# Trace of a batched matrix product: the order of five-row and twelve-row loads

## The chip, the cores and the metric

The kernel runs on one core of a Trainium2 chip. The metric is the device time of one execution in microseconds (us).

## The reference

```python
B, N = 8, 2176
a, b = randn(B, N, N), randn(B, N, N)          # float32

def reference(a, b):
    prod = np.matmul(a, b)
    traces = np.diagonal(prod, axis1=1, axis2=2).sum(axis=-1)
    return traces.astype(np.float32)           # 8 numbers
```

No product of matrices is needed: the trace of A B is the sum over all i, k of A[i, k] B[k, i], so each batch is an elementwise product of A transposed with B, summed. Both inputs, 2 x 8 x 2176 x 2176 float32 or 303 MB, have to be read once.

## The kernel before, in words

**Rows and tiles.** A matrix has 17 row tiles of 128 rows. They are held in three groups of 6, 6 and 5: in a group with m rows a partition holds m neighbouring rows of the matrix, so that a load is one long run in each partition. `a_six` and `b_six` hold the first two groups (twelve rows a partition) of A and of B, and **one** buffer, `five`, holds the last group of A and, later, the last group of B. `at` holds A transposed. All four are single buffers in bf16. In what follows a "row" is one such row tile, 128 x 2176, and a load has twelve, six or five rows.

**Loads.** POOL issues all loads but one, with a cast from float32 to bf16 on the way, into a single queue. Its program is a list written by hand: waits and `fetch` calls (L179) in a fixed order. In batch 0 the first row of A comes over SP's queue as float32 into the space of `b_six` (`words`) and is cast by ScalarE and VectorE. The waits that free the buffers are: `made` (TensorE has transposed so many tiles) ahead of a load over A's rows, and `product` (VectorE has finished so many products) ahead of a load over B's. `five` changes hands twice a batch: A's five rows go in after the product with B's five rows, B's five rows after all tiles of A's five rows are made.

**TensorE** runs the same program for each batch: 26 tiles (`EACH`), each of them up to 16 transposes into one of three PSUM slots (L224 for pairs of bf16 columns moved as float32, L227 for bf16). The 18 tiles of the twelve rows come first (`HEAD` = 18), then the 8 tiles of the five rows. It waits on `moved` at tiles 0 and `HEAD`; SP waits for the loads of A in that order and posts the counts (L173).

**Emptying the slots.** ScalarE copies three tiles of four from PSUM to `at` (L269), VectorE the fourth (L295). Before its first tile of a batch each waits for both products of the batch before, as these still read `at`.

**Products.** VectorE multiplies and sums `at` with B (L284): with the twelve rows of B, then with the five.

**The last batch.** B arrives in nine pieces (`pieces`), the twelve rows as 6, 4 and 2, the five as 2, 1, 1 and three parts of a row. VectorE takes some pieces, TensorE others as matrix products whose diagonals add up in `trace_ps` (L253); filler matmuls (L255) lie between these. Then the parts are summed, and SP stores the eight results.

The order of POOL's issues before is, for batch n: A's twelve rows, A's five rows, B's twelve rows, B's five rows.

Of the kernel before, what the change touches and what calls it, by code (L numbers as in the profile page):

```python
# [21 lines left out]
def kernel(  # L22
# [7 lines left out]
    P = 128  # L30
    BATCH, N, N2 = a.shape
    assert N == N2 and N % P == 0
    NT = N // P
    SIX, FIVE = 6, 5
    TWICE = 2 * SIX
    assert TWICE + FIVE == NT
    LAST = BATCH - 1
# [12 lines left out]
    a_six = big.tile([P, TWICE, N], bf16, tag="a_six")  # L50
    b_six = big.tile([P, TWICE, N], bf16, tag="b_six")
    five = big.tile([P, FIVE, N], bf16, tag="five")
# [14 lines left out]
    def tiles_of(rows, start, m):  # L67
# [31 lines left out]
    six_tiles = [  # L99
        t for g in range(2)  # L100
        for t in tiles_of(a_six[:, g * SIX:(g + 1) * SIX, :], g * SIX * P, SIX)
    ]
    five_tiles = list(tiles_of(five, TWICE * P, FIVE))
    tiles = six_tiles + five_tiles
    EACH, HEAD = len(tiles), len(six_tiles)
    on_vector = [n for n in range(EACH) if n % 4 == 3]
    on_scalar = [n for n in range(EACH) if n % 4 != 3]

    def flat(t):
        return t.rearrange("p r k -> p (r k)")  # L110

    def six(src):
        return src[0:TWICE * P, :].rearrange("(g p r) k -> p g (r k)", g=2, r=SIX)

    def rows_of(src, start, m, r0, r1):
        return src[start:start + P * m, :].rearrange("(p r) k -> p (r k)", r=m)[:, r0 * N:r1 * N]

    by_twos = "p (g r) k -> p g (r k)"
# [29 lines left out]
    with tc.tile_critical(no_gpsimd_drain=True) as section:  # L148
        def counted(name):
            return Counted(nc, name)  # L150

        first_row, first_five = counted("first_row"), counted("first_five")
        d_a6, d_a5, d_b6, d_b5 = (counted(f"load_{x}") for x in ("a6", "a5", "b6", "b5"))
        d_late = [counted(f"late{n}") for n in range(len(pieces))]
        zeros, ready, cast = counted("zeros"), counted("ready"), counted("cast")
        moved, made = nc.alloc_semaphore("moved"), nc.alloc_semaphore("made")
        free = [nc.alloc_semaphore(f"free{k}") for k in range(SLOTS)]
        scalar_done, vector_done = counted("scalar_done"), counted("vector_done")
        product, early, added = counted("product"), counted("early"), counted("added")
# [3 lines left out]

        sp = nc.sync
        words = flat(b_six[:, 0:2, :].bitcast(f32))
        first_row.by(sp.dma_start(out=words, in_=rows_of(a[0], 0, SIX, 0, 1)), 16)
        for n in range(BATCH):
            if n == 0:
                sp.wait_ge(cast.sem, 2)
                sp.wait_ge(first_five.sem, 16)  # L170
            for load in (d_a6, d_a5):
                sp.wait_ge(load.sem, 16 * (n + 1))
                sp.sem_inc(moved)  # L173


        gp = nc.gpsimd

        def fetch(count, dst, src):
            count.by(gp.dma_start(out=dst, in_=src), 16)  # L179

        for n in range(BATCH):
            if n == 0:
                fetch(first_five, flat(a_six[:, 1:SIX, :]), rows_of(a[0], 0, SIX, 1, SIX))
                fetch(d_a6, flat(a_six[:, SIX:, :]), rows_of(a[0], SIX * P, SIX, 0, SIX))
                gp.wait_ge(zeros.sem, 2)
                for t in (identity32, identity16):
                    ready.by(gp.affine_select(
                        out=t, in_=t, compare_op=mybir.AluOpType.not_equal, fill=1.0, base=0,
                        pattern=[[-1, P]], channel_multiplier=1,
                    ))  # L190
            else:
                gp.wait_ge(made, EACH * (n - 1) + HEAD)
                fetch(d_a6, a_six.rearrange(by_twos, g=2), six(a[n]))
                gp.wait_ge(product.sem, 2 * n)
            fetch(d_a5, flat(five), rows_of(a[n], TWICE * P, FIVE, 0, FIVE))
            if n == 0:
                gp.wait_ge(cast.sem, 2)
            else:
                gp.wait_ge(product.sem, 2 * n - 1)
            if n < LAST:  # L200
                fetch(d_b6, b_six.rearrange(by_twos, g=2), six(b[n]))
                gp.wait_ge(made, EACH * (n + 1))
                fetch(d_b5, flat(five), rows_of(b[n], TWICE * P, FIVE, 0, FIVE))
                continue
            for k, piece in enumerate(pieces):
                if piece.v0 == TWICE:
                    gp.wait_ge(made, EACH * (n + 1))
                fetch(d_late[k], piece.dst, piece.src)
        gp.drain()


        pe = nc.tensor
# [2 lines left out]
            pe.sem_inc(free[k])  # L215
        with pe.Fori(0, BATCH):
            for n, (moves, _, _) in enumerate(tiles):
                if n in (0, HEAD):
                    pe.wait_ge(moved, 1).then_inc(moved, -1)
                ps = slots[n % SLOTS]  # L220
                pe.wait_ge(free[n % SLOTS], 1).then_inc(free[n % SLOTS], -1)  # L221
                for dtype, place, src in moves:
                    if dtype == f32:
                        last = pe.transpose(ps[:, place, :], src, identity32)  # L224
                    else:
                        ps16 = ps.bitcast(bf16).rearrange("q a b -> q (a b)")
                        last = pe.transpose(ps16[:, place * P:(place + 1) * P], src, identity16)  # L227
                last.then_inc(made, 1)
# [18 lines left out]
        for w in work:  # L247
            k, x, y = w
# [10 lines left out]
        middle = N // 2  # L259
        act = nc.scalar  # L260
        act.wait_ge(first_row.sem, 16)
        cast.by(act.copy(out=a_six[:, 0, :middle], in_=words[:, :middle]))  # L262
        for n in range(BATCH):
            for t in on_scalar:
                _, dst, view = tiles[t]
# [10 lines left out]
        dve = nc.vector  # L276
# [1 line left out]
        for t in (identity32, identity16):  # L278
            zeros.by(dve.memset(t, 0.0))
        dve.wait_ge(first_row.sem, 16)  # L280
        cast.by(dve.tensor_copy(out=a_six[:, 0, middle:], in_=words[:, middle:]))  # L281

        def multiply_reduce(x, y, acc, out=None):
            return dve.tensor_tensor_reduce(  # L284
                out=x if out is None else out, in0=x, in1=y, scale=1.0, scalar=0.0,
                op0=MUL, op1=ADD, accum_out=acc,
            )

        for n in range(BATCH):
            for t in on_vector:  # L290
                _, dst, view = tiles[t]
                if t == on_vector[0] and n:
                    dve.wait_ge(product.sem, 2 * n)
                dve.wait_ge(made, EACH * n + t + 1)
                ins = dve.tensor_copy(out=dst, in_=view(slots[t % SLOTS]))  # L295
                if t != on_vector[-1]:
                    ins.then_inc(free[t % SLOTS], 1)
                else:
                    vector_done.by(ins)
            dve.wait_ge(vector_done.sem, n + 1).then_inc(free[on_vector[-1] % SLOTS], 1)  # L300
            dve.wait_ge(scalar_done.sem, n + 1).then_inc(free[on_scalar[-1] % SLOTS], 1)
            if n == LAST:
                continue
            for k, (load, t, v0) in enumerate(((d_b6, b_six, 0), (d_b5, five, TWICE))):
                dve.wait_ge(load.sem, 16 * (n + 1))
                product.by(multiply_reduce(
                    flat(at[:, v0:v0 + t.shape[1], :]), flat(t), sums[:, 2 * n + k:2 * n + k + 1],
                ))
        dve.wait_ge(early.sem, 1)
        dve.reduce_sum(  # L310
            out=result[:1, 0:LAST],
            in_=total[:, 0:2 * LAST].rearrange("o (b n) -> o b n", n=2),
# [3 lines left out]
        for k, (piece, (lo, hi, _)) in enumerate(zip(pieces, shares)):  # L316
            if hi > lo:
                dve.wait_ge(d_late[k].sem, 16)
                t, base = (b_six, 0) if piece.v0 < TWICE else (five, TWICE)
# [11 lines left out]
        for c in range(cols):  # L331
# [9 lines left out]
            out=out.rearrange("(a b) -> a b", a=1), in_=result[:1, :],  # L341
# [40 lines left out]
```

## Time and profile before

| | |
|---|---|
| median of 3 runs | 709.66 us (709.39 to 709.72) |
| profiled execution | 709.2 us, its span 707.1 us |
| busy share: VectorE, ScalarE, TensorE, POOL | 54%, 29%, 26%, 4% |
| POOL's queue, share of 16 DMA engines | 99.7%, 7552 packets, 150.96 MB written |
| read from HBM | 303.04 MB, 429 GB/s over the span |
| product with twelve rows of B, with five | 27.36 us, 11.48 us |
| granted TensorE clock, mean | 0.671 |

The span runs from the first to the last instruction. In the profile PE is TensorE, PEld its weight loads, DVE VectorE, ACT ScalarE, POOL GpSimd and SP SyncE, and L179 is line 179 of the kernel. Instructions that issue a DMA are not counted as busy time of the engine; a DMA's own time is on the queues. "idle before <-" names what ended the time in which an engine waited.

### The profile page before, as it was taken

The page shows a single profiled execution, that of the slowest core. Times are in us where ns is not written, and L with a number is a line of the kernel's source. Part 1 is how long each engine was busy: PE and PEld are TensorE (multiplying, and loading weights), DVE is VectorE, ACT ScalarE, POOL GpSimd, SP SyncE. Part 2 cuts the span into 40 slices and gives each one's busy share as a digit, 9 for nine tenths or more (in the row PEclk, how much of TensorE's full clock was granted, in tenths as well). Part 3 has the DMA queues.
Part 4 walks back from the last instruction along what each step waited for, and adds up shares of the span by engine and source line. Part 5 has one row for each costly group of instructions (what it writes and reads, how often), then busy time and mean ns, then how long its engine had stood idle before and what let it go on. Part 6 is the DMA issues. An engine that isn't in the chain of part 4 may idle for free. (4 is left out here: it accounts for less than half of the span.)

```text
span 707.1 us, 3879 instructions
## 1 busy us (share of the span) xinstructions
PE 182.3 (26%) x1611; PEld 164.0 (23%) x1613; DVE 380.7 (54%) x94; ACT 203.8 (29%) x162; POOL 24.9 (4%) x46
## 2 busy tenths in 40 slices
PE   0083000830018200182002710028100371003706
PEld 0073000730017200172002610027000370003704
DVE  0031596315963169541794407944089340894487
ACT  1095000950009400093001930019200292003910
POOL 1000000000000000000000000000000000001010
PEclk9998555885559755597555965559655596555957
DMA  9999999999999999999999999999999999999997
GB/s 221 222 219 212 213 228 203 216 219 216 219 215 220 219 215 217 211 217 222 220 213 217 220 217 214 220 213 221 217 215 213 219 222 213 220 219 213 218 209 152
DMA packets 7702, 152.13 MB, mean 215 GB/s; under 512 B 658, under 2 KB 914, under 8 KB 1298
## 3 DMA queue, kind: packets, MB, share of 16 engines
q0 software_dynamic: 7552, 150.96, 99.7%
q1 hardware_dynamic: 146, 1.11, 0.5%
q8 instruction: 2, 0.03, 0.0%
q14 instruction: 2, 0.02, 0.0%
HBM read 303.04 MB, written 0.00 MB: 429 GB/s over the span
## 5 line engine op out<-in xcount | busy, mean ns | idle before, releaser
L269 ACT COPY at<-aT 128x1536 bf16<-128x1536 bf16 (+3 forms) x160 | 201.4, 1367 | 465.5 <-PE aT L224 465.1
L284 DVE CUSTOM_DVE_ANT_0 at<-at,b_six 128x26112 bf16<-128x26112 bf16 (+2 forms) x9 | 214.4, 23831 | 130.9 <-DMA b_six<-in_b_dram 130.9
L224 PE MATMUL aT<-identity,a_six 128*128 128x128 f32 x576 | 91.6, 324 | 482.6 <-PEq L221 482.6
L224 PEld LDWEIGHTS aT<-identity,a_six 128*128 128x128 f32 x576 | 85.4, 207 | 488.1 <-issue 487.8
L295 DVE COPY at<-aT 128x1536 bf16<-128x1536 bf16 (+1 forms) x48 | 80.1, 1669 | 182.7 <-PE aT L224 152.0
L284 DVE CUSTOM_DVE_ANT_0 at<-at,five 128x10880 bf16<-128x10880 bf16 (+3 forms) x10 | 85.0, 8501 | 1.6 <-DMA five<-in_b_dram 1.6
L227 PE MATMUL aT<-identity,a_six 128*128 128x128 bf16 x480 | 33.5, 219 | 11.6 <-PEq L221 11.4
L224 PE MATMUL aT<-identity,five 128*128 128x128 f32 x240 | 34.6, 289 | 4.4 <-PEq L221 4.4
L227 PEld LDWEIGHTS aT<-identity,a_six 128*128 128x128 bf16 x480 | 29.3, 118 | 15.5 <-issue 15.4
L224 PEld LDWEIGHTS aT<-identity,five 128*128 128x128 f32 x240 | 30.4, 198 | 7.4 <-issue 7.0
L179 POOL DMA_DIRECT2D five<-in_a_dram x8 | 4.4, 556 | 389.0 <-DVE sums L284 389.0
L179 POOL DMA_DIRECT2D five<-in_b_dram x13 | 7.1, 555 | 256.5 <-PE aT L227 256.5
L227 PE MATMUL aT<-identity,five 128*128 128x128 bf16 x200 | 13.9, 219 | 2.8 <-PEq L221 1.8
L227 PEld LDWEIGHTS aT<-identity,five 128*128 128x128 bf16 x200 | 11.9, 118 | 5.1 <-issue 5.1
L253 PE MATMUL trace_ps<-b_six,at 128*128 128x128 bf16 x34 | 3.8, 310 | 18.3 <-DMA b_six<-in_b_dram 18.3
L253 PEld LDWEIGHTS trace_ps<-b_six,at 128*128 128x128 bf16 x34 | 3.5, 145 | 18.4 <-issue 18.4
L179 POOL DMA_DIRECT2D b_six<-in_b_dram x10 | 6.6, 662 | 3.6 <-ACT a_six L262 3.6
L179 POOL DMA_DIRECT2D a_six<-in_a_dram x9 | 6.2, 687 | 1.0 <-SPq L148 1.0
L253 PE MATMUL trace_ps<-five,at 128*128 128x128 bf16 x54 | 3.8, 220 | 2.6 <-DMA five<-in_b_dram 2.4
L253 PEld LDWEIGHTS trace_ps<-five,at 128*128 128x128 bf16 x54 | 3.0, 98 | 4.4 <-DMA five<-in_b_dram 4.3
L255 PE MATMUL aT<-at 128*128 128x512 bf16 x13 | 3.7, 412 | 0.3 <-issue 0.2
L281 DVE CAST a_six<-b_six 128x1088 bf16<-128x1088 f32 x1 | 0.7, 726 | 4.7 <-DMA b_six<-in_a_dram 4.7
(19 smaller groups left out, 8.6 us busy)
## 6 DMA issues: line engine op xcount, KB each, us to landing
b_six<-in_b_dram POOLq DMA_DIRECT2D x7, 6528.0 KB, 47.7
a_six<-in_a_dram POOLq DMA_DIRECT2D x7, 6528.0 KB, 60.9
five<-in_a_dram POOLq DMA_DIRECT2D x8, 2720.0 KB, 17.4
five<-in_b_dram POOLq DMA_DIRECT2D x7, 2720.0 KB, 30.7
a_six<-in_a_dram POOLq DMA_DIRECT2D x1, 3264.0 KB, 32.1
b_six<-in_b_dram POOLq DMA_DIRECT2D x1, 3264.0 KB, 32.3
a_six<-in_a_dram POOLq DMA_DIRECT2D x1, 2720.0 KB, 17.3
b_six<-in_b_dram POOLq DMA_DIRECT2D x1, 2176.0 KB, 42.0
```

The source lines that it names most:

```text
L179: count.by(gp.dma_start(out=dst, in_=src), 16)
L224: last = pe.transpose(ps[:, place, :], src, identity32)
L227: last = pe.transpose(ps16[:, place * P:(place + 1) * P], src, identity16)
L253: ins = pe.matmul(trace_ps, x, y, start=w is real[0], stop=w is real[-1])
L255: pe.matmul(slots[0][:, 0:4, :], x, y, start=True, stop=True)
L269: ins = act.copy(out=dst, in_=view(slots[t % SLOTS]))
L281: cast.by(dve.tensor_copy(out=a_six[:, 0, middle:], in_=words[:, middle:]))
L284: return dve.tensor_tensor_reduce(out=x if out is None else out, in0=x, in1=y, scale=1.0, scalar=0.0, op0=MUL, op1=ADD, accum_out=acc,)
L295: ins = dve.tensor_copy(out=dst, in_=view(slots[t % SLOTS]))
```

## The change

For each batch the five-row loads are issued ahead of the twelve-row loads, for A and for B: A's five, A's twelve, B's five, B's twelve. TensorE's tiles follow: the 8 tiles of the five rows first (`HEAD` = 8), then the 18 of the twelve. VectorE multiplies with B's five rows first. In batch 0 SP's row is now the first of A's five, POOL loads the other four and then all twelve rows in one load (before: five, six, five). In the last batch A's twelve rows come as two loads of six, and TensorE waits a third time in each batch, at tile 17 (`SECOND`), for the second of them; in the other batches SP posts two counts when the twelve rows have landed. The waits ahead of each load are changed to suit: A's five rows wait for the first product of the batch before, A's twelve for all its tiles, B's five for the first eight tiles of this batch, B's twelve for the second product of the batch before.

```diff
--- before.py
+++ after.py
@@ -101,8 +101,9 @@
         for t in tiles_of(a_six[:, g * SIX:(g + 1) * SIX, :], g * SIX * P, SIX)
     ]
     five_tiles = list(tiles_of(five, TWICE * P, FIVE))
-    tiles = six_tiles + five_tiles
-    EACH, HEAD = len(tiles), len(six_tiles)
+    tiles = five_tiles + six_tiles
+    EACH, HEAD = len(tiles), len(five_tiles)
+    SECOND = HEAD + len(six_tiles) // 2
     on_vector = [n for n in range(EACH) if n % 4 == 3]
     on_scalar = [n for n in range(EACH) if n % 4 != 3]
 
@@ -149,8 +150,9 @@
         def counted(name):
             return Counted(nc, name)
 
-        first_row, first_five = counted("first_row"), counted("first_five")
+        first_row = counted("first_row")
         d_a6, d_a5, d_b6, d_b5 = (counted(f"load_{x}") for x in ("a6", "a5", "b6", "b5"))
+        d_half = [counted(f"half{g}") for g in range(2)]
         d_late = [counted(f"late{n}") for n in range(len(pieces))]
         zeros, ready, cast = counted("zeros"), counted("ready"), counted("cast")
         moved, made = nc.alloc_semaphore("moved"), nc.alloc_semaphore("made")
@@ -163,50 +165,61 @@
 
         sp = nc.sync
         words = flat(b_six[:, 0:2, :].bitcast(f32))
-        first_row.by(sp.dma_start(out=words, in_=rows_of(a[0], 0, SIX, 0, 1)), 16)
+        first_row.by(sp.dma_start(out=words, in_=rows_of(a[0], TWICE * P, FIVE, 0, 1)), 16)
+
+
+
+        gp = nc.gpsimd
+        arrivals = []
+
+        def fetch(count, dst, src, opens=0):
+            reached = count.by(gp.dma_start(out=dst, in_=src), 16)
+            if opens:
+                arrivals.append((count.sem, reached, opens))
+
         for n in range(BATCH):
             if n == 0:
-                sp.wait_ge(cast.sem, 2)
-                sp.wait_ge(first_five.sem, 16)
-            for load in (d_a6, d_a5):
-                sp.wait_ge(load.sem, 16 * (n + 1))
-                sp.sem_inc(moved)
-
-
-        gp = nc.gpsimd
-
-        def fetch(count, dst, src):
-            count.by(gp.dma_start(out=dst, in_=src), 16)
-
-        for n in range(BATCH):
+                fetch(d_a5, flat(five[:, 1:FIVE, :]), rows_of(a[0], TWICE * P, FIVE, 1, FIVE), 1)
+            else:
+                gp.wait_ge(product.sem, 2 * n - 1)
+                fetch(d_a5, flat(five), rows_of(a[n], TWICE * P, FIVE, 0, FIVE), 1)
+                gp.wait_ge(made, EACH * n)
+            if n < LAST:
+                fetch(d_a6, a_six.rearrange(by_twos, g=2), six(a[n]), 2)
+            else:
+                for g in range(2):
+                    fetch(
+                        d_half[g], flat(a_six[:, g * SIX:(g + 1) * SIX, :]),
+                        rows_of(a[n], g * SIX * P, SIX, 0, SIX), 1,
+                    )
             if n == 0:
-                fetch(first_five, flat(a_six[:, 1:SIX, :]), rows_of(a[0], 0, SIX, 1, SIX))
-                fetch(d_a6, flat(a_six[:, SIX:, :]), rows_of(a[0], SIX * P, SIX, 0, SIX))
                 gp.wait_ge(zeros.sem, 2)
                 for t in (identity32, identity16):
                     ready.by(gp.affine_select(
                         out=t, in_=t, compare_op=mybir.AluOpType.not_equal, fill=1.0, base=0,
                         pattern=[[-1, P]], channel_multiplier=1,
                     ))
-            else:
-                gp.wait_ge(made, EACH * (n - 1) + HEAD)
-                fetch(d_a6, a_six.rearrange(by_twos, g=2), six(a[n]))
-                gp.wait_ge(product.sem, 2 * n)
-            fetch(d_a5, flat(five), rows_of(a[n], TWICE * P, FIVE, 0, FIVE))
-            if n == 0:
-                gp.wait_ge(cast.sem, 2)
-            else:
-                gp.wait_ge(product.sem, 2 * n - 1)
             if n < LAST:
+                gp.wait_ge(made, EACH * n + HEAD)
+                fetch(d_b5, flat(five), rows_of(b[n], TWICE * P, FIVE, 0, FIVE))
+                if n == 0:
+                    gp.wait_ge(cast.sem, 2)
+                else:
+                    gp.wait_ge(product.sem, 2 * n)
                 fetch(d_b6, b_six.rearrange(by_twos, g=2), six(b[n]))
-                gp.wait_ge(made, EACH * (n + 1))
-                fetch(d_b5, flat(five), rows_of(b[n], TWICE * P, FIVE, 0, FIVE))
                 continue
+            gp.wait_ge(product.sem, 2 * n)
             for k, piece in enumerate(pieces):
                 if piece.v0 == TWICE:
-                    gp.wait_ge(made, EACH * (n + 1))
+                    gp.wait_ge(made, EACH * n + HEAD)
                 fetch(d_late[k], piece.dst, piece.src)
         gp.drain()
+
+
+        sp.wait_ge(cast.sem, 2)
+        for sem, reached, opens in arrivals:
+            sp.wait_ge(sem, reached)
+            sp.sem_inc(moved, opens)
 
 
         pe = nc.tensor
@@ -215,7 +228,7 @@
             pe.sem_inc(free[k])
         with pe.Fori(0, BATCH):
             for n, (moves, _, _) in enumerate(tiles):
-                if n in (0, HEAD):
+                if n in (0, HEAD, SECOND):
                     pe.wait_ge(moved, 1).then_inc(moved, -1)
                 ps = slots[n % SLOTS]
                 pe.wait_ge(free[n % SLOTS], 1).then_inc(free[n % SLOTS], -1)
@@ -259,7 +272,7 @@
         middle = N // 2
         act = nc.scalar
         act.wait_ge(first_row.sem, 16)
-        cast.by(act.copy(out=a_six[:, 0, :middle], in_=words[:, :middle]))
+        cast.by(act.copy(out=five[:, 0, :middle], in_=words[:, :middle]))
         for n in range(BATCH):
             for t in on_scalar:
                 _, dst, view = tiles[t]
@@ -278,7 +291,7 @@
         for t in (identity32, identity16):
             zeros.by(dve.memset(t, 0.0))
         dve.wait_ge(first_row.sem, 16)
-        cast.by(dve.tensor_copy(out=a_six[:, 0, middle:], in_=words[:, middle:]))
+        cast.by(dve.tensor_copy(out=five[:, 0, middle:], in_=words[:, middle:]))
 
         def multiply_reduce(x, y, acc, out=None):
             return dve.tensor_tensor_reduce(
@@ -301,7 +314,7 @@
             dve.wait_ge(scalar_done.sem, n + 1).then_inc(free[on_scalar[-1] % SLOTS], 1)
             if n == LAST:
                 continue
-            for k, (load, t, v0) in enumerate(((d_b6, b_six, 0), (d_b5, five, TWICE))):
+            for k, (load, t, v0) in enumerate(((d_b5, five, TWICE), (d_b6, b_six, 0))):
                 dve.wait_ge(load.sem, 16 * (n + 1))
                 product.by(multiply_reduce(
                     flat(at[:, v0:v0 + t.shape[1], :]), flat(t), sums[:, 2 * n + k:2 * n + k + 1],
```

## The prediction

> **What bounds the kernel now.** I read the page first: engine shares, slices, queues. The columns of the slices are fortieths of the span, 17.7 us each.
>
> ```profile
> span 707.1 us, 3879 instructions
> ...
> DVE  0031596315963169541794407944089340894487
> ...
> DMA  9999999999999999999999999999999999999997
> GB/s 221 222 219 212 213 228 203 216 219 216 219 215 220 219 215 217 211 217 222 220 213 217 220 217 214 220 213 221 217 215 213 219 222 213 220 219 213 218 209 152
> ...
> q0 software_dynamic: 7552, 150.96, 99.7%
> ```
>
> No compute engine reaches 60% of the span (VectorE 54%, the most), while the DMA row holds 9 in all slices but the last and one queue, POOL's, fills 99.7% of 16 engines' time. So the bytes bound the kernel, and an edit can gain only where that queue runs dry, or ahead of its first byte, or behind its last. Next the chain of waits of the end, in order of time:
>
> ```profile
> 672.25 2.08 POOL five L179 x4
> 674.33 29.41 DMA five<-in_b_dram
> 703.74 0.04 issue
> 703.79 0.61 PE trace_ps L253 x6
> ```
>
> The last pieces of B are issued at 672.25 and land at 703.74, behind others in the queue. About 3.3 us follow to the end of the span (707.06 - 703.74): last matmuls, trace, store.
>
> Then the timeline around the issues of batch 1, to see how full the queue is when POOL refills it (start, duration, idle before):
>
> ```profile
> 106.19 11.48 DVE L284 CUSTOM_DVE_ANT_0 at<-at,five 128x10880 bf16<-128x10880 bf16 x1
> 117.60 0.08 DVE L284 DVE_READ_ACCUMULATOR2_ANT sums<- 128x1 f32 x1
> 117.97 0.56 POOL L179 DMA_DIRECT2D five<-in_a_dram  x1 [56.24 <-DVE sums L284]
> 118.53 0.71 POOL L179 DMA_DIRECT2D b_six<-in_b_dram  x1
> 122.85 0.30 PEld L224 LDWEIGHTS aT<-identity,a_six 128*128 128x128 f32 x2 [62.84 <-issue]
> 122.88 0.45 PE L224 MATMUL aT<-identity,a_six 128*128 128x128 f32 x1 [62.72 <-PEq L221]
> ```
>
> PE starts as the twelve rows of A land (122.88). The five-row load behind them was issued at 117.97, a **lead** of 4.91 us. In the batches after it the same two rows give 4.91 (210.33 - 205.42), 4.91, 4.91, 4.86, 4.88, 4.86. Is that enough? The windows between these issues:
>
> ```profile
> 117.90:205.40 87.50, 21.65 (x187) 19.87 (x187) 48.79 (x10) 25.21 (x20) 2.53 (x4) 0.64 1.01 215
> 205.40:292.70 87.30, 20.96 (x187) 19.05 (x187) 48.79 (x10) 25.12 (x20) 2.53 (x4) 0.64 1.01 217
> 292.70:380.00 87.30, 21.53 (x187) 19.62 (x187) 48.79 (x10) 25.21 (x20) 2.53 (x4) 0.64 1.01 217
> ```
>
> A batch takes 87.45 us from issue to issue the first time (205.42 - 117.97), then 87.29; DMA share is 1.01. So 34 rows of tiles cost 87.29 us: 2.567 a row, 12.84 for a five-row load, 15.40 for six, 30.81 for twelve. A lead of 4.9 is just enough: the trace's packet records show packets of the late five-row load starting 2.7 us after its issue in batch 1, as the twelve-row load's packets run out.
>
> **The bytes.** Before, batch 0's A is 1 + 5 + 6 + 5 rows, after it 1 + 4 + 12: both 17. The last batch's twelve rows become 6 + 6. Loads: before 6 + 6x4 + 11 = 41, after 5 + 6x4 + 12 = 41. Every packet is a run of one partition, and the packet records have a fixed time per size (26,112 bytes 1942 ns, 21,760 1622, 17,408 1302, which is 320 ns a row and 22 more). Batch 0 has three groups of packets either way, 1622 + 1942 + 1622 = 5186 before and 1302 + 2 x 1942 = 5186 after. Cost 0.
>
> **The start.** SP's first row and POOL's first load keep their places ahead of all else; the first POOL load is shorter by one row, 2.57 us, and the twelve-row load behind it is issued within 1.2 us of it (the two first issues take 1.20). POOL now issues batch 0's loads of B only when the five-row tiles of A are made: those rows land at about 34.3 - 15.4 - 2.6 = 16.3 (the first twelve rows landed at 34.3; six rows and one less), and the tiles take 7.3 (below), so at about 24 instead of 7.39. What hides this is the queue: it holds 17 rows, 44 us, from the beginning. Without that cover it would cost about 17 us once. Cost 0.
>
> **The steady batches.** Let b be the landing of B's twelve rows of the batch before.
> - *Issue of B's five rows.* The next A, 17 rows, lands at b + 43.98 (122.88 - 78.90). VectorE now does the short product first, so the long one runs from b: 27.36 and 0.08. Only then may ScalarE and VectorE write `at`, so the five rows of A, which land at b + 13, wait about 14 us and gain nothing by being early. TensorE has three slots filled by then. Eight five-row tiles took 7.3 us from PE's first (53.16) to the issue that waited for them (60.46); with three tiles ready I take the same 7.3 as the upper end and ScalarE's five copies of 1.27 to the slot of tile 7, 6.4, as the lower. Issue at b + 27.4 + 0.4 + 7.3 = b + 35.1. Lead 43.98 - 35.1 = 8.9 us, where 4.9 was just enough. B's twelve rows follow 0.6 us later: the product they wait for is over.
> - *Issue of A's five rows.* From the landing of A's twelve rows, 18 tiles take 18.3 us (34.68 to 53.0), ScalarE's last copy 2.0, the short product 11.48, POOL 0.4: 32.2. B lands at 43.47 (166.35 - 122.88). Lead 11.3 us. The twelve rows of A follow at once, since all tiles were transposed before that product.
>
> Both leads are about double those of before. What can be gained is what the queue lost: at least nothing, at most the dip in slice 6, (217 - 203)/217 x 17.7 = 1.1 us; by the periods 87.45 - 87.29 = 0.16, and 0.27 over all six (641.98 - 117.97 = 524.01 against 6 x 87.29 = 523.74). I take -0.3, near the periods, since single slices scatter by 10 GB/s.
>
> **The rule against it.** When the eighth five-row tile is made, POOL issues B's loads while VectorE copies that tile; no issue inside a batch of before lies under a VectorE instruction. The copies take 1492 ns for 1280 elements and 1758 for 1536, 1.04 ns an element. If such a copy held the issue up, it would take at most 1.49 of the 8.9 us, which leaves 7.4; that decides nothing alone, and together with slower tiles it is 2 of the 7 in 100 of rival 1. The Trainium skill, "SBUF — State Buffer", section "SBUF: two separate sides", says that GpSimd cannot write the descriptors of its DMAs while VectorE runs an instruction in a mode that takes both ports. By it, too, the sum would stay where it is; no row here shows such a stall.
>
> **PE's waits.** A third wait, at tile 17, is added to each batch; but for the last, SP posts two counts when the twelve rows land, so it finds its count at once. SP's own waits stand in order of arrival, with nothing of its own queued behind them but the final store. Cost 0.
>
> **The last batch.** A's last load lands at 659.4 in both:
>
> ```profile
> L173 SPq EVENT_SEMAPHORE  x16: 17/17/28, 34.3 to 659.4; - x16
> ```
>
> After, that load is six rows: nine tiles, 9.2 us, and 2.0 for ScalarE give 670.6, where before VectorE was free at 674.2 and the first piece of B landed at 674.8. So VectorE again waits for the load. Had the twelve rows stayed one load, it would be 659.4 + 18.3 + 2.0 = 679.7, 4.9 late, and VectorE's pieces (13.8, 9.2, 2.4, 1.4, 0.8 us, with 1.6 us of waits between them: 1.0, 0.2, 0.4) would end some 3 us late: the split hides that. The pieces of B keep order and size; they are issued from about 642 on, the five-row ones about 649 instead of 672.25, with the queue full. Cost 0, and behind the last byte nothing changes.
>
> **Sum.** 709.2 (the profiled execution; its span and 2.1 around it) - 0.3 = 708.9. The median of the runs is 0.46 above that execution: 709.4.
>
> **Rivals.**
> 1. *The queue runs dry at B's five-row load.* Place: POOL's wait for the eighth tile, behind a 27.4 us product. It decides when the product and tiles together end later than b + 39, that is if the eight tiles take over 11.3 us rather than 7.3. For it: PE's clock is 0.5 after its idle time, and this load had not stood behind the long product. Against: 36 transposes took 6.92 us from a cold start in batch 1, and ScalarE's copies, not PE, set the pace. Each us too late costs seven batches 7 us: one us gives 716.4. 7 in 100.
> 2. *The gaps were larger than the periods show*, and the lead of 4.9 cost the queue a little in every batch. For: slice 6. Against: 87.29 comes again to 0.1 us in five batches, with no slice like it. Full dip 1.1: 708.6. If each of seven batches lost 0.4 us: 709.66 - 2.8 = 706.9. 15 in 100 for the first kind, which is still within 0.2%; 6 for the second.
> 3. *One DMA engine falls behind elsewhere.* From 34.68 to 122.88, 34 rows too, took 88.20, 0.9 above 87.29. The packet records show two instruction packets of 16 KB beside the loads, 935 and 974 ns, at 54 and 694. Who is last at the end depends on which engine they hit: both on one, up to 1.0 more, 710.4. 12 in 100; no rival of size, but the upper end of the range.
> 4. *The change does not do what it says*: the five rows come early, but `at` is not free. I count this as certain, and it is in the sum.
>
> **Numbers.** Sum as it stands, or within half a us of it, 57 in 100; large dip 15, engine behind 12: these 84 are within 0.2% (1.42 us), which is about what a measurement of this kernel can tell from no change. Slower: rival 1 with 7, and 3 for what I have not seen, 10. Faster 6. The range goes from the full dip, 708.5, to the sum with an engine 1.0 behind and 0.3 for gaps that stay, 710.7.
>
> **What would show it.** In the profile after: DMA 9 in all slices but the last; a period of 87.3 between POOL's issues; POOL waiting for PE before B's five rows, with a lead of some 9 us, and 11 us at A's five rows; VectorE idle ahead of the long product, not the short; the last landing near 703.5. Wrong if VectorE's long product starts at intervals above 87.5 (rival 1), below 87.1 (rival 2), or if PE's last transposes pass 674.

## The result and the profile after

The change makes the kernel faster by about a microsecond: 708.11 us (707.97 to 708.24, 20 runs) against 709.21 us (708.36 to 709.72, 20 runs). The ratio is 0.9985 with a 95% interval of 0.9979 to 0.9991, which is 0.6 to 1.5 us. That is within the 0.2% called no change, but below the low end of the range, 708.5. The runs also lie closer together: 0.27 us from lowest to highest instead of 1.36.

The page of the profiled execution after (708.12 us, span 706.0), the same lines:

```profile
span 706.0 us, 3887 instructions
...
DVE  0105488054871549715396163961639616395477
...
DMA  9999999999999999999999999999999999999997
GB/s 225 225 208 211 226 214 215 216 225 213 216 227 213 206 219 221 215 213 227 209 218 228 210 210 226 214 215 214 226 207 219 228 207 214 224 217 215 213 213 159
...
q0 software_dynamic: 7552, 150.96, 99.7%
```

The queue is as full as before by this view: packets, bytes and share are the same. The slices scatter more than before (206 to 228 without the last), though nothing runs dry any more, and the first experiment below, in which nothing runs dry either, has 205 in the very slice that reads 203 before. So that slice, on which the bound of 1.1 us rested, is no measure of a gap. The chain of waits of the end, in order of time:

```profile
650.50 1.56 POOL five L176 x3
652.06 49.97 DMA five<-in_b_dram
702.03 0.05 issue
702.08 0.51 PE trace_ps L266 x6
702.59 0.07 another core or an unknown queue
702.66 0.04 issue
702.70 0.62 PE trace_ps L266 x6
```

The last wait for a piece of B that the chain shows ends at 702.66 instead of 703.74, and that is the whole gain: span 706.0 instead of 707.1. (Both chains merge the wait for the very last piece into the matmuls; it lands at 702.98 and 704.06, also 1.08 us apart.) B's five-row pieces are issued at 650.50, not 672.25, and wait 50 us in the queue.

The timeline at the two places where the queue is refilled, first B's loads of batch 1:

```profile
121.85 1.49 DVE L308 COPY at<-aT 128x1280 bf16<-128x1280 bf16 x1 [2.82 <-PE aT L237]
...
125.58 1.49 DVE L308 COPY at<-aT 128x1280 bf16<-128x1280 bf16 x1 [2.25 <-PE aT L240]
125.84 0.56 POOL L176 DMA_DIRECT2D five<-in_b_dram  x1 [45.14 <-PE aT L240]
126.41 0.71 POOL L176 DMA_DIRECT2D b_six<-in_b_dram  x1
135.61 2.43 PEld L237 LDWEIGHTS aT<-identity,a_six 128*128 128x128 f32 x12 [10.22 <-issue]
135.64 2.59 PE L237 MATMUL aT<-identity,a_six 128*128 128x128 f32 x11 [10.09 <-PEq L234]
```

then A's loads of batch 2:

```profile
167.95 0.56 POOL L176 DMA_DIRECT2D five<-in_a_dram  x1 [40.84 <-DVE sums L297]
168.51 0.71 POOL L176 DMA_DIRECT2D a_six<-in_a_dram  x1
178.94 27.36 DVE L297 CUSTOM_DVE_ANT_0 at<-at,b_six 128x26112 bf16<-128x26112 bf16 x1 [11.29 <-DMA b_six<-in_b_dram]
```

The leads are 9.80 us (135.64 - 125.84; 8.7 to 10.0 in the six batches) and 10.99 us (178.94 - 167.95), where there was one of 4.9. VectorE now waits 11.3 us ahead of the long product and none of it matters.

What the page can't show is in the trace's records of single packets. A packet of a five-row load, 21,760 bytes, takes 1622 ns. Just after POOL's late five-row load of A reached the queue in batch 1, at 120.7 us of the kernel before, 18 of them took 1680 to 2624 ns. I read this as a dry spell: DMA engines had run out of packets and waited for the new ones. Each row sums what such stretched packets took above 1622 ns and divides it by the 16 engines:

```
                      excess per DMA engine, us (time of the spell)
before                0.40 (120.7)  0.05 (208.3)  0.04 (295.6)  0.02 (644.9)
after                 none at any refill
```

### The profile page after: what moved, and what is told of

The parts are those of the page before. It is cut to its first block, busy times and chain, and to the rows that moved or that the text cites. A ratio compares the mean times of both kernels' runs of the same rounds, so it can differ in the third digit from the quotient of the medians.

```text
span 706.0 us, 3887 instructions
## 1 busy us (share of the span) xinstructions
PE 203.7 (29%) x1611; PEld 184.7 (26%) x1613; DVE 381.4 (54%) x94; ACT 204.9 (29%) x162; POOL 25.1 (4%) x46
## 3 DMA queue, kind: packets, MB, share of 16 engines
q0 software_dynamic: 7552, 150.96, 99.7%
q1 hardware_dynamic: 146, 1.11, 0.5%
## 5 line engine op out<-in xcount | busy, mean ns | idle before, releaser
L237 PE MATMUL aT<-identity,five 128*128 128x128 f32 x240 | 54.7, 418 | 367.7 <-PEq L234 367.7
L237 PEld LDWEIGHTS aT<-identity,five 128*128 128x128 f32 x240 | 47.0, 221 | 373.6 <-issue 373.6
L240 PE MATMUL aT<-identity,five 128*128 128x128 bf16 x200 | 17.1, 260 | 0.1
L240 PEld LDWEIGHTS aT<-identity,five 128*128 128x128 bf16 x200 | 16.8, 132 | 0.7 <-issue 0.3
```

## The experiments

Theory: the lead of 4.9 us is at the edge, the queue runs dry there, and the longer leads of the change prevent it. Rival: the gain lies in batch 0's loads, in the last batch's order or in where packets of code fall. Medians of the kernel before in the four groups of runs: 708.84 (first two experiments), 709.13 (next four), 708.87 and 708.63.

**The old order with a longer lead.** Only the size of the long product is changed:

```diff
+                rows = 10 if k == 0 else t.shape[1]
...
-                    flat(at[:, v0:v0 + t.shape[1], :]), flat(t), sums[:, 2 * n + k:2 * n + k + 1],
+                    flat(at[:, v0:v0 + rows, :]), flat(t[:, 0:rows, :]),
+                    sums[:, 2 * n + k:2 * n + k + 1],
```

> The kernel before, its loads and tiles in the old order; VectorE's long product leaves out two of the twelve rows of B (4.6 us shorter), so that the lead of A's five-row load grows from 4.9 to 9.5 us. Theory (the queue ran dry at that load, and engines that ran dry lost up to 1 us): faster than before by what the change gained, 0.7 to 1.2 us. Rival (the gain lies in batch 0's loads or in the last batch's order, not in the lead): within 0.2 us of before.

708.20 us, ratio 0.9989 (0.9980 to 0.9998), all runs from 707.98 to 708.31: the time of the kernel after, and its narrow spread, with none of its order. No stretched packets at any refill. So the start and the last batch of the change add nothing to the gain that can be measured, and the lead is the cause.

**The same in batch 0 alone** (`rows = 10 if k == 0 and n == 0`).

> The kernel before; two of the twelve rows are left out of the long product in batch 0 alone, so that only batch 1's five-row load of A is issued 4.6 us earlier. Theory: the dry spell at 120.7 us is by far the largest, so this has most of the gain, 0.5 to 1.0 us. If instead every batch lost a little: a seventh of the gain, 0.15 us. Rival (start or end of the kernel): nothing.

708.92 us, ratio 0.9999 (0.9990 to 1.0008): no gain, a miss. The trace says where it went. In batch 1 the lead is long, in batch 2 it is 4.91 again:

```profile
113.43 0.56 POOL L179 DMA_DIRECT2D five<-in_a_dram  x1 [52.19 <-DVE sums L284]
...
122.87 1.52 PE L224 MATMUL aT<-identity,a_six 128*128 128x128 f32 x6 [63.19 <-PEq L221]
```
```profile
205.25 0.56 POOL L179 DMA_DIRECT2D five<-in_a_dram  x1 [55.65 <-DVE sums L284]
...
210.16 3.23 PE L224 MATMUL aT<-identity,a_six 128*128 128x128 f32 x14 [62.12 <-PEq L221]
```

The stretched packets are gone at 120.7 and stand at 208.1 us instead (0.19 us an engine). The spell is not tied to batch 1; it comes at the first refill with the short lead. (This execution took 708.25 us and is one of the faster of its 11 runs, so its spell need not be what the median lost.) The reason is in the landings, where each of the 16 DMA engines posts its own count. In before, one engine falls 1.0 us behind the other 15 after a packet of code (16 KB, 935 ns, at 54 us, in the profile's queue q8): for A's twelve rows of batch 1, 15 counts come from 120.99 to 121.57 us and the last at 122.56. VectorE's product starts when that last engine has landed, so POOL's refill is late by 1.0 us for the other 15. Once they have run dry they stand closer to the laggard (five of them within 0.6 us of it at the next landing), and later refills cost less.

**A lead longer by 1.2 us**, the size of that lag (long product without 1150 of its 26112 elements):

> The kernel before; the long product leaves out 1150 of 26112 elements, about 1.2 us, so that the lead grows from 4.9 to 6.1 us. In the traces one DMA engine lags the rest by 1.0 us after a packet of code, and the product starts when that engine has landed, so that the other 15 run dry once by up to 1.0 us less what the lead has to spare. Theory: 1.2 us more are just enough to cover that lag, and the kernel comes to within 0.3 us of the one with the lead of 9.5 (708.2). Rival (every batch wants a long lead): at most a third of that gain.

708.13 us, ratio 0.9987 (0.9978 to 0.9996).

```profile
116.91 0.56 POOL L179 DMA_DIRECT2D five<-in_a_dram  x1 [54.89 <-DVE sums L284]
...
123.01 1.31 PE L224 MATMUL aT<-identity,a_six 128*128 128x128 f32 x5 [62.56 <-PEq L221]
```

A lead of 6.1 us is enough for the whole gain, and its trace has no stretched packets at the refills. Leads of 9 and 11 us buy no more.

**A shorter lead, in the old order and in the new.** Ahead of the second product of a batch (`k == 1`), VectorE does a spare one, of 800 elements in the old order and of 4352 in the new:

```diff
+                if k == 1:
+                    x = flat(t)[:, 0:SPARE]
+                    multiply_reduce(x, x, late[:, 7:8], out=spare)
```

> The kernel before; ahead of each short product VectorE squares 800 elements of B's five rows into a spare tile, about 1.0 us, so that the lead of A's five-row load falls from 4.9 to about 3.9 us in seven batches. Theory (4.9 is just enough, and the loss counts once for an engine that lags but in every batch for a lead that is short for all engines): 0.8 to 1.0 us a batch, 5 to 7 us slower than before. Rival (the lead has slack for most engines): within 0.5 us of before.

716.57 us (4 runs), ratio 1.0111 (1.0095 to 1.0128), 7.4 us slower. Windows from issue to issue of A's five rows:

```profile
118.80:207.30 88.50, 21.15 (x187) 19.24 (x187) 49.71 (x12) 25.12 (x20) 2.53 (x4) 0.63 1.02 218
207.30:295.90 88.60, 21.33 (x187) 19.39 (x187) 49.71 (x12) 25.13 (x20) 2.53 (x4) 0.63 1.01 214
295.90:384.50 88.60, 21.39 (x187) 19.45 (x187) 49.71 (x12) 25.18 (x20) 2.54 (x5) 0.63 1.00 214
384.50:473.50 89.00, 21.45 (x187) 19.49 (x187) 49.71 (x12) 25.21 (x20) 2.52 (x4) 0.63 1.00 213
```

From issue to issue the six batches take 88.50, 88.60, 88.51, 89.14, 88.22 and 87.39 us, where 87.29 is due without a loss: leads of 3.9 to 4.0 us cost 1.1 us a batch on average, about the microsecond by which the lead was cut, but 0.1 to 1.9 in single batches. So the edge is near 4.9: below it the queue loses in nearly every batch, at it mainly once, and 6.1 is enough although one engine lags.

> The kernel after; ahead of each long product VectorE squares two rows of B's twelve into a spare tile, about 4.7 us, so that the lead of B's five-row load falls from 8.7 to 10.0 us to 4.0 to 5.3 us. Theory (the same edge of about 4.9 us holds for this load): the gain is lost again and some more, 1 to 4 us slower than after. Rival (the gain lies at the start or the end of the kernel): as after.

710.35 us (708.86 to 714.59), ratio to before 1.0028 (1.0013 to 1.0044), 2.2 us above the median of after. The six leads are 4.90, 4.46, 5.62, 4.92, 4.22 and 5.16 us. Stretched packets are back at 133.6 us (0.92 us an engine) and 221.4 (0.49); there are none at the refill with 5.62, and at each of the last three they add up to 0.06 or less. So a short lead at this load costs time as well. But the lead alone does not give the size of a spell: 4.22, the shortest, came after two spells and cost 0.03, where 3.9 in the old order kept costing about 1 us.

**Without the split of the last A load.**

```diff
-            if n < LAST:
-                fetch(d_a6, a_six.rearrange(by_twos, g=2), six(a[n]), 2)
-            else:
-                for g in range(2):
...
+            fetch(d_a6, a_six.rearrange(by_twos, g=2), six(a[n]), 2)
```

> The kernel after with the last batch's twelve rows of A in one load again. By the sum of the prediction VectorE is free for the first piece of B some 4.9 us after it has landed and ends some 3 us later than after. Rival (TensorE's share and the queue still end last): within 0.3 us of after.

711.36 us, 3.25 above after; ratio to before 1.0038 (1.0024 to 1.0052). VectorE's timeline:

```profile
679.12 0.16 DVE L315 TENSOR_REDUCE result<-total 1x7 f32<-1x14 f32 x1 [2.01 <-ACT at L274]
679.21 13.75 DVE L289 CUSTOM_DVE_ANT_0 at<-at,b_six 128x13056 bf16<-128x13056 bf16 x1
692.88 0.08 DVE L289 DVE_READ_ACCUMULATOR2_ANT late<- 128x1 f32 x1
692.88 9.22 DVE L289 CUSTOM_DVE_ANT_0 at<-at,b_six 128x8704 bf16<-128x8704 bf16 x1
```

With the split, in after, it waited for the first piece:

```profile
674.46 13.76 DVE L297 CUSTOM_DVE_ANT_0 at<-at,b_six 128x13056 bf16<-128x13056 bf16 x1 [4.97 <-DMA b_six<-in_b_dram]
```

Without it the first piece starts at 679.21, and from there VectorE no longer waits for a load: it has become the bound of the end.

**The second packet of code.** In the profiled execution of before, a 16 KB packet of 974 ns at 694 us hit an engine that the dry spell had set back: from first to last, the 16 counts of a piece spread over 1.27 us ahead of it and over 2.0 behind it. That engine's landing ended the kernel. If this were how the loss reaches the end, a TensorE program too short to need the packet should end earlier. The edit leaves pieces out of TensorE's share:

```diff
             mine = []
+            if k in (2, 3):
+                continue
```

> The kernel before without TensorE's 68 matmuls for pieces 2 and 3 and their 13 fillers, so that its program is some 160 instructions shorter and should need no second packet of code at 694 us; those four rows of B are left out of the last trace. Theory (the dry spell sets engines back by up to 1 us, and the kernel's end shows it when the second code packet, 0.97 us, hits one of them): the end comes 0.4 to 1.0 us earlier than before, near the kernel after, and the runs lie closer together. Rival (the code packet is hidden): within 0.2 us of before, with the same spread.

> The kernel after without the same 81 matmuls of TensorE. Theory: one engine is still 0.9 us behind from the first code packet, so the end comes only 0 to 0.2 us earlier than after. Rival (the second packet alone sets the end of after): 0.7 to 1.0 us earlier.

These two did not make the case they were built for: the packet was still needed, only later, at 702.6 and 701.4 us. 708.76 us, ratio 1.0001 (0.9992 to 1.0010), and 708.24 us, ratio 0.9989 (0.9980 to 0.9998), so nothing follows. With pieces 2, 3, 5, 6 and 7 left out, one packet of code before the end is left:

```profile
q8 instruction: 1, 0.02, 0.0%
```

> The kernel before with only piece 8 (and no filler) left of TensorE's share of the last batch: its program is some 40 instructions shorter still than with pieces 2 and 3 left out, so that the second packet of code, which came at 702.6 us there, should not be needed before the end. Pieces 2, 3 and parts of 5, 6 and 7 are left out of the last trace. Theory (the end of before shows an engine that the dry spell set back and that this packet then hits): 0.4 to 0.9 us earlier than before, the last landing near 703.0 instead of 703.8. Rival (the packet does not reach the end, or what it costs is hidden): within 0.2 us of before.

> The kernel after with the same part of TensorE's share left out. Theory: the engine that lags from the first packet of code still lands at 702.6, so 0 to 0.2 us earlier than after. Rival (the second packet alone sets the end of after): 0.7 to 1.0 us earlier.

708.82 us, ratio 0.9998 (0.9988 to 1.0008), runs from 707.94 to 710.53; and 708.22 us, ratio 0.9990 (0.9981 to 0.9999). The old order is as slow and as scattered without the second packet as with it. From the last landing to the end of the span it takes 3.18 us in both, instead of 3.00 in before and 3.01 in after, so that some 0.2 us of a gain could hide there, but not the 0.4 to 0.9 that the theory asked for. My reading of the one execution does not hold for the median: this part of the theory fell. What remains is the dry spell itself, whose size differs from run to run; the packet matters in no median here.

## Why the prediction was right or wrong, point by point

**What was right.** The bytes bound both kernels. The leads: 8.9 us forecast for B's five rows, 8.7 to 10.0 measured; 11.3 for A's, 10.99 measured in batch 2. The batch still takes 87.3 us (178.94 - 91.66 = 87.28 between starts of the long product, then 87.29). Batch 0's loads of B are issued at 24.57 us (about 24), long before the queue's loads of A run out: the last of these land at 46.99. VectorE is free at 669.34 in the last batch (670.6) and waits 4.97 us for the first piece. The split hides 3.25 us (some 3). Coming early gains the five rows of A nothing, since `at` is not free: ScalarE waits 51.6 us for the product in batch 1.

**The step that failed: the size of what the queue lost.** The prediction held a lead of 4.9 us to be "just enough" and took -0.3 "near the periods", between 0 and 1.1. The kernels with a longer lead are faster in their medians by 0.6 (9.4 us), 1.0 (6.1 us) and 1.1 us (the change, with an interval of 0.6 to 1.5). The lead was enough for the slowest engine only, and the periods could not show more. They run from landing to landing, and a load has landed when the slowest of 16 engines has: that engine was the laggard. In batch 1 of before the last of the 16 counts is 0.15 us late, the 16 on average 0.5: the late load's counts come on average 13.37 us after those of the load ahead, where 12.86 pass with a longer lead. A period of 87.45 where 87.29 was due, in the very batch where the lead first mattered, was the sign, and the text had the packet records that show some 0.5 us of the loss.

**The second term: the base.** Adding 0.46 because the median of three runs lay above the profiled execution was wrong by as much. In 20 runs before's median is 709.21, the profiled execution's own 709.2; those three runs were among its slowest, and a kernel that runs dry by chance scatters. Without that term, and with 1.1 for the gaps, the sum is 708.1.

**Rivals.** Rival 2 in its first form, gaps larger than the periods show, is what happened. That its 1.1 us equals the measured gain is luck: it was read from a slice that reads as low where nothing runs dry. Rival 1 has its edge near where the prediction put it, a lead of 4.9, and its price was near, measured at the other load (1.0 us too late: 7 us forecast, 7.4 measured), but the change stays 4 us clear of it. Rival 3's engine fell behind as feared, 1.0 us after the packet of code at 57.8 us. The 88.20 us that this rival started from are that lag: in before, the last of the 16 counts stands 0.05 us behind the next one at 34.23 us and 0.99 behind at 122.56. But both kernels have it, and with full queues it is no addition.

**The rule against the change.** In after the issue at 125.84 lies under VectorE's copy of 125.58 to 127.07. It had 9.8 us to spare, so nothing can be read from it. Where the lead was cut to 4.90 the issue also lay under such a copy and its spell was 0.92 us, more than the 0.40 of before at 4.91; that is one spell against one. Two later refills of the same run speak against the copy. With leads of 4.46 and 4.22, under such copies too, the load's first packets are recorded 1.92 and 1.94 us after the issue. The copies end 1.23 us after it, and with a dry queue and no copy (the kernel with the shorter lead) the shortest time from issue to first packet is 1.25 us. Had the issue been held to the end of the copy, some 2.5 us would have passed; a shorter hold is not excluded. In before, one issue lay under a VectorE instruction after all, the last piece's at 674.85 under the product from 674.82, with the queue full.

**What stays open.** Per engine, the stretched packets of the profiled execution of before add up to about 0.5 us, while the median gain is 1.1. The counts of the 16 engines account for the rest in the two profiled executions. The last piece lands on average at 702.68 us before and at 702.05 after, 0.63 us apart, and the last of its 16 counts stands 1.38 us behind that average before and 0.93 after, 0.45 more: together the 1.08 us between 704.06 and 702.98. Other executions divide it otherwise; in the old order without the second packet of code the average is 702.98 and the last count 0.57 behind it. Why the spells of one kernel differ so much between runs, these runs do not settle.

## What to carry to other kernels

A queue whose share of busy time reads 99.7% can still lose time at each refill: compare the moment of each issue with the moment at which the load ahead of it lands, and learn from a run with a shorter and one with a longer lead where the edge is. A lead that is just enough by the landings is not enough when one engine lags, since the landing and the issue wait for the slowest and the others run dry; here 1.2 us more was worth as much as 5. Periods between landings see only the slowest engine and hide what the other 15 lose.

## What was not expected of the hardware

A load that reaches an empty queue starts slowly: with a lead of 3.9 us the first packets of most refills are recorded 1.25 to 1.27 us after POOL's issue, but take 2.0 to 2.6 us instead of 1.62, so that the loss is larger than the gap between packets. One packet of code, 16 KB and 0.94 us, put one of 16 DMA engines 1.0 us behind for the rest of the kernel: in after, its counts come 1.15 us later than those of the middle engines at 60.85 us and still 1.11 us later at 689.93. Every load waits for a count from each of the 16 engines, and as long as the queue stayed full nothing in these traces evened out the lag; only dry spells did.
